# A block of three MLPs on one core: SBUF tiles at other addresses, and the MLP's first matrices with the high and the low part of x side by side in one 512-column matmul

## The chip, the core and the metric

The kernel runs on one core of a Trainium2 chip. The metric is the device time of one execution in microseconds (us), the median of several runs.

## The reference

One token block of 256 rows and 1024 columns in float32 passes through three layers. The first has a convolution branch, a stick-breaking attention and a cross attention to a memory, and then an MLP; the other two have attention, retention and an MLP. The three MLPs compute the same form, and the change's new matmuls are in them alone:

```python
h2 = rms_norm(x, g_mlp[l])
x = x + jnp.square(jax.nn.relu(h2 @ w_up[l])) @ w_down[l]
...
hid = jnp.square(jax.nn.relu(jnp.einsum('bsd,df->bsf', x, w_ff1)))
ff = jnp.einsum('bsf,fd->bsd', hid, w_ff2)
return layernorm(DEEPNORM_ALPHA * x + ff, ln2_g, ln2_b)
```

The first matrix (`w_up`, `w_ff1`) is 1024 x 4096, the second (`w_down`, `w_ff2`) 4096 x 1024.

## The kernel before, in words

**Three matmuls for one product.** Each operand is split into a high part (rounded to float32r, by ACT) and a low part (what is left, by DVE). A product is high x high + high x low + low x high: `mm3`, lines 319 to 322, so the trace shows each product as three matmuls, of lines 320, 321 and 322. The names in a matmul's row are the moving operand first and the weights (the stationary operand) second: `acc<-xTh,whi` streams `xTh` past weights from `whi`.

**Weights come as a stream.** `Stream` (lines 164 to 232) walks a fixed plan of 196 chunks of 1024 x 256 or 512 x 512 weights. A chunk comes in two halves: a DMA of 512 KB into one of five `raw` buffers (`load`, line 190, on SP's queue), a cast by ACT to `whi` (line 213) and a subtraction by DVE to `wlo` (line 214). There are five buffers of each, and in the MLPs a sixth pair that is lent (`lend`). `tick` puts one half (`pump`) in the order of ACT and DVE after each unit of matmuls, so that three chunks or more lie ahead of PE. The order on each engine is the order of the program text; no scheduler changes it.

**Two shapes of unit.** `unit_b` (line 340) has the activations as weights and streams 512 columns of `whi` or `wlo`: 4 steps of k, 12 matmuls of 512 columns. `unit_a` (line 335) has a 128 x 128 block of `whi` or `wlo` as weights and streams the 256 tokens of `xTh` or `xTl`: 8 steps of k, 24 matmuls of 256 columns. `stream_a` (line 347) does two such units, the halves of one PSUM bank `acc` (four banks go round).

**An MLP** (`mlp`, line 789): the first 1024 columns of the first matrix go by `unit_b`. Then for each group g from 2 to 7 there are two chunks of the first matrix by `stream_a`; ACT takes relu out of the bank and squares (lines 800, 801), `split` (line 311) makes the two parts of `hid[g]`, and four units `down` of the second matrix use `hid[g - 2]`. A program has 36 such chunks, 3 x 6 x 2, with 36 x 2 x 8 = 576 products of 256 columns.

**Where tiles lie.** Pools are stacked from low addresses (side "left") or from the top (side "right"), each tile on a multiple of 32 bytes. In the kernel before, small tiles of 4 to 96 bytes stand ahead of large ones. The starts (bytes in a partition) as the built programs have them, and what is left of them after division by 256:

| tiles | before | rest | changed | rest |
|---|---|---|---|---|
| `whi`, five, 8448 apart | 38176 | 32 | 17408 | 0 |
| `wlo`, five, 8448 apart | 80416 | 32 | 59648 | 0 |
| lent `whi`, `wlo` | 182176, 190624 | 160 | 180736, 189184 | 0 |
| `xTh`, `xTl` (changed: one `xT`) | 130848, 139040 | 32 | 110080 | 0 |
| `hid`, `ych`, `memTh`, `mTh`, `osbh`, `oxh` and their low parts | from 149408 | 160 | from 147968 | 0 |
| `mixh`, `mixl` | 149440, 157632 | 192 | 147968, 156160 | 0 |
| `ident` (moving operand of transposes) | 16512 | 128 | 16896 | 0 |

A step of k moves an operand by 1024 or 2048 bytes, which keeps the rest, but for 96 matmuls of 264 columns (k steps of 1056 bytes). Counted in the program before, among float32r matmuls of 128 rows: of 2,936 with 512 columns, 1,247 stream an operand with the same rest as the weights that the next matmul needs, and 1,689 one with another; 3,418 have 256 columns (1,728 of them in the 576 products above). No moving operand of float32r starts on a multiple of 128 bytes, but for some of those with 264 columns.

Of the kernel before, what the change touches and what calls it, by code (L numbers as in the profile page):

```python
# [9 lines left out]
F32 = mybir.dt.float32  # L10
F32R = mybir.dt.float32r
# [9 lines left out]
RB = 5  # L21
# [218 lines left out]
def block_kernel(ctx: ExitStack, tc: tile.TileContext, a: dict, out: bass.AP, upto=None, dbg=None):  # L240
# [3 lines left out]
    def pool(stack, name, bufs=1, side="left", space=None):  # L244
        kw = {} if space is None else {"space": space}
        return stack.enter_context(tc.tile_pool(name=name, bufs=bufs, side=side, reuse_waits="tile", **kw))

    kp = pool(ctx, "const")
    rp = pool(ctx, "raw", RB)
    wp = pool(ctx, "wts", NB)  # L250
    ap = pool(ctx, "act")
    accp = pool(ctx, "acc", 4, space=bass.MemoryType.PSUM)
    psum = ExitStack()
    ctx.push(psum)
    cur_ps = [None]
    sm = pool(ctx, "small", 4)

    def acc():
        return accp.tile([128, 512], F32, tag="acc", name="acc")
# [80 lines left out]
    def unit_b(o, w, t, x, k0=0, first=True, last=True):  # L340
        nk = w[0].shape[1]
        ts = slice(t * 128, t * 128 + 128)
        for k in range(nk):
            mm3(o, x[0][:, k0 + k, ts], x[1][:, k0 + k, ts], w[0][:, k, :], w[1][:, k, :],
                first and k == 0, last and k == nk - 1)

    def stream_a(key, x):
        w = W.get(key)
        p = acc()
        pv = p.rearrange("p (n t) -> p n t", n=2)  # L350
        unit_a(pv[:, 0, :], w, 0, x)
# [27 lines left out]
        (nc.sync, nc.scalar)[h].dma_start(xt[:, 0, 512 * h:512 * h + 512], xsrc[:, 0, 512 * h:512 * h + 512])  # L379
    gmix = ph0.tile([128, D], F32, name="gmix")  # L380
    nc.sync.dma_start(gmix, a["g_mix"][0].partition_broadcast(128))
    ident = kp.tile([128, 128], F32, name="ident")
    nc.scalar.dma_start(ident, a["c1"][:, 0:128])
    W.load(2)
    nc.sync.dma_start(xt[:, 1, :], xsrc[:, 1, :])
    W.load()
    mh = kp.tile([128, 4], F32, name="mh")
    nc.gpsimd.memset(mh, -0.5)
    wz = ph0.tile([128, 512], BF16, name="wz")
    nc.vector.memset(wz, 0.0)  # L390
# [26 lines left out]
        stt(dst, src, rs, gb, ALU.mult, ALU.mult)  # L417

    def new_xT():
        return (ap.tile([128, 8, S], F32R, tag="xTh", name="xTh"), ap.tile([128, 8, S], F32R, tag="xTl", name="xTl"))  # L420


    hT = new_xT()
    ht = [ph0.tile([128, D], F32, name=f"ht{t}") for t in range(2)]
    ss = sm.tile([128, 2], F32, tag="ss2", name="ss2")
    rs = sm.tile([128, 1], F32, tag="rs", name="rs")
    for h in range(2):
        hs = slice(512 * h, 512 * h + 512)
# [46 lines left out]
    dmask = sp.tile([128, 128], F32, name="dmask")  # L475
    nc.gpsimd.dma_start(smask, a["c1"][:, 128:896])
    nc.gpsimd.dma_start(dmask, a["c1"][:, 896:1024])
    cw = sp.tile([128, 8, 3], F32, name="cw")
    nc.gpsimd.dma_start(cw, a["conv_w"])
    qs = tuple(sp.tile([128, 2, S], F32R, name=f"q{i}") for i in range(2))  # L480
    kb = tuple(sp.tile([128, 2, S], F32R, name=f"kb{i}") for i in range(2))
    u = sp.tile([128, 2, S + 2], F32, name="u")
    nc.vector.memset(u[:, :, 0:2], 0.0)

    yc = ycur("yc")
# [261 lines left out]
    def rms_half(t, n, bank, xtok, gb, dst, xT, cell):  # L747
        ns = slice(512 * n, 512 * n + 512)
        if n == 0:
            cell[t] = sm.tile([128, 2], F32, tag="ss2", name="ss2")  # L750
        tt(xtok[:, t, ns], bank, xtok[:, t, ns], ALU.add)
        nc.scalar.activation(dst[:, ns], xtok[:, t, ns], AF.Square, accum_out=cell[t][:, n:n + 1])
        if n == 1:
            ss = sm.tile([128, 1], F32, tag="ss", name="ss")
            rs = sm.tile([128, 1], F32, tag="rs", name="rs")
            tt(ss, cell[t][:, 0:1], cell[t][:, 1:2], ALU.add)
            rstd_of(rs, ss, 1, 1.0 / D, EPS)
            stt(dst, xtok[:, t, :], rs, gb, ALU.mult, ALU.mult)
            sides.append(late_T(dst, xT, t))
# [29 lines left out]
    def mlp(tag, xT, half, on_start):  # L789
        st = ExitStack()  # L790
        tmp = lambda: hp.tile([128, D], F32, tag="r", name="r", bufs=2)
        hp = pool(st, "mlp" + str(tag))
        W.lend(pool(st, "wts" + str(tag)), (tag, "dn", 7, 1))
        hid = {}

        def new_hid(g):
            hid[g] = tuple(hp.tile([128, 4, S], F32R, tag=f"hid{i}", name=f"hid{i}", bufs=3) for i in range(2))

        def relu2(dst, src):
            nc.scalar.activation(dst, src, AF.Relu)  # L800
# [12 lines left out]
        ws = [(n, j, W.get((tag, "up", n, j))) for n in range(2) for j in range(2)]
        new_hid(0)
        new_hid(1)
        for t in range(2):
            p = [bank(), bank()]
            r = hp.tile([128, D], F32, tag="r", name="r", bufs=2)
            for n, j, w in ws:
                unit_b(p[n], w, t, xT, 4 * j, j == 0, j == 1)  # L820
                if t == 1:
                    W.free()
                if j:
                    relu2(r[:, 512 * n:512 * n + 512], p[n])
                    if n:
                        sides.append(tok_side(t, r))
                tick(1)
            if t == 0:
                on_start(st)
        pd = None  # L830

        def down(g, n, t, w):
            unit_b(pd[t][n], w, t, hid[g], 0, g == 0, g == 7)

        for g in range(2, 8):
            new_hid(g)
            for cc in range(2):
                p = stream_a((tag, "up", 2 * g + cc), xT)
                r = hp.tile([128, D], F32, tag="r", name="r", bufs=2)
                rv = r[:, 0:512].rearrange("p (n t) -> p n t", n=2)  # L840
                relu2(rv, p)
                split(hid[g][0][:, 2 * cc:2 * cc + 2, :], hid[g][1][:, 2 * cc:2 * cc + 2, :], rv)
                tick()
            if pd is None:
                pd = [[bank(), bank()] for _ in range(2)]
            for n in range(2):
                w = W.get((tag, "dn", g - 2, n))
                for t in range(2):
                    down(g - 2, n, t, w)
                    if t == 1:  # L850
                        W.free()
                    tick()
        ws = [(W.get((tag, "dn", g, n)), g, n) for n in range(2) for g in (6, 7)]
        for t in range(2):
            for w, g, n in ws:
                down(g, n, t, w)
                if t == 1:
                    W.free()
                if g == 7:
                    half(t, n, pd[t][n], tmp)  # L860
# [17 lines left out]

    def open_b2(st):
        st4.close()  # L880
        cp = pool(b2, "c2", side="right")
        for nm, sh, dt in (("cst", [128, C2W], F32), ("sel", [128, 8, 128], F32R), ("chl", [128, S], F32R),
                           ("gnp", [128, 2, 4], F32)):
            c2s[nm] = cp.tile(sh, dt, name=nm)
# [27 lines left out]
    def ln_half(t, n, bank, xtok, gb, bb, xT, cell, tmp, fin=None):  # L912
        ns = slice(512 * n, 512 * n + 512)
        if n == 0:
            cell[t] = sm.tile([128, 2], F32, tag="lsum", name="lsum")
        nc.vector.scalar_tensor_tensor(out=xtok[:, t, ns], in0=xtok[:, t, ns], scalar=ALPHA, in1=bank, op0=ALU.mult,
                                       op1=ALU.add, accum_out=cell[t][:, n:n + 1])
        if n == 0:
            return
        nm = sm.tile([128, 1], F32, tag="nm", name="nm")  # L920
        ss = sm.tile([128, 1], F32, tag="ss", name="ss")
        rs = sm.tile([128, 1], F32, tag="rs", name="rs")
        nc.vector.tensor_scalar(nm, cell[t][:, 0:1], cell[t][:, 1:2], -1.0 / D, op0=ALU.add, op1=ALU.mult)
# [14 lines left out]
    for l in range(2):  # L938
# [3 lines left out]
        def T(shape, dt, tag, bufs=1):  # L942
            return p2.tile(shape, dt, tag=tag, name=tag, bufs=bufs)

        bf = T([128, 8], F32, "bf")
        nc.gpsimd.dma_start(bf, a["b_forget_2"][l].partition_broadcast(128))
        mix = (T([128, 8, S], F32R, "mixh"), T([128, 8, S], F32R, "mixl"))


        qr = T([128, 2, 512], F32, "ta")  # L950
        kr = T([128, 2, 512], F32, "tb")
        fy = T([128, 2, 8], F32, "fy")

        def rotary(dst, src, t):
            nh = src.shape[1] // 128
# [34 lines left out]
           cc_("zeta").unsqueeze(2).to_broadcast([128, 4, 128]), ALU.mult)  # L990


        fa = T([128, 2, 8], F32, "fa")
        act_set(EXPLN)
        nc.scalar.activation(fa, fy, AF.Abs)
        nc.scalar.activation(fa, fa, AF.Exp, scale=-1.0)
# [48 lines left out]
        def fox_pair(g, nt, z_at, e_at, t_at, pv_at):  # L1045
# [10 lines left out]
                    mm(zb[:, h, :], sel[64 * h:64 * h + 40, 2 * pair + h, :], chl[64 * h:64 * h + 40, 0:nk], False, True)  # L1056
            zd = z[:, :, 128:384].rearrange("p h (b k) -> p h b k", b=2)
            tt(zd, zd, cc_("neg").unsqueeze(1).unsqueeze(1).to_broadcast([128, 2, 2, 128]), ALU.add)
            mx = sm.tile([128, 4], F32, tag="fmx", name="fmx")
            nc.vector.tensor_reduce(mx[:, 0:2], z[:, :, 0:256], AX.X, ALU.max)  # L1060
            nc.vector.tensor_reduce(mx[:, 2:4], z[:, :, 256:384], AX.X, ALU.max)
            nc.vector.tensor_scalar(mx, mx, -1.0, None, op0=ALU.mult)
# [62 lines left out]
        def ret_side():  # L1125
# [139 lines left out]
```

## Time and profile before

| what | value |
|---|---|
| median of 3 runs | 1223.83 us (1223.82 to 1224.01) |
| profiled execution | 1223.95 us, span 1222.1 us |
| PE busy | 1208.5 us, 99% of the span, 7365 matmuls |
| DVE busy | 734.8 us, 60% |
| ACT busy | 631.6 us, 52% |
| HBM | 178 GB/s over the span |
| chain that ended last | PE 95% |

The span is the time from the first to the last instruction; the execution's own time is 1.85 us longer. A matmul's row in the trace has a start and a duration; the durations overlap (a matmul of 256 columns lasts 0.28 us and the next starts 0.12 us after it), so the pace is read from the distance of starts.

### The profile page before, as it was taken

Reading aid. Unit: us, or ns where it says so; the run is one execution under the profiler, and the core shown is the slowest. Engines: PE = TensorE matmul, PEld = TensorE weight load, DVE = VectorE, ACT = ScalarE, POOL = GpSimd, SP = SyncE. Lnnn points to the kernel's source line nnn. Section 1 sums busy time; section 2 is a strip of 40 time slices with the busy share of each in tenths; the row PEclk is TensorE's granted clock in tenths of the full one; section 3 lists DMA queues with packets and bytes.
Section 4 is the critical chain, followed back from the end, with each engine's and each line's share of the span. In section 5 each row is a group of like instructions: output and inputs, shape, how many; then the busy total and the mean of one; then the engine's idle time right before and its main releaser. Section 6 shows DMA issues by size and latency. Waiting matters only on the chain.

```text
span 1222.1 us, 18186 instructions
## 1 busy us (share of the span) xinstructions
PE 1208.5 (99%) x7365; PEld 1059.1 (87%) x7365; DVE 734.8 (60%) x941; ACT 631.6 (52%) x887; POOL 26.2 (2%) x45
## 2 busy tenths in 40 slices
PE   8999999999999999999999999999999999999997
PEld 5999987887888888998898889899889888989985
DVE  6488775656666655355476685535567668553452
ACT  6556555545454565455255556545535555653540
POOL 1000000000000000000000100000000010000000
PEclk9999999999999999999999999999999999999999
DMA  8644446665455565556444366555545436655530
GB/s 327 224 148 144 140 156 211 233 195 162 138 172 189 184 243 208 172 172 214 156 166 139 124 214 226 197 188 173 207 130 187 146 118 216 225 193 203 167 126 35
DMA packets 60468, 218.99 MB, mean 179 GB/s; under 512 B 6848, under 2 KB 6992, under 8 KB 60384
## 3 DMA queue, kind: packets, MB, share of 16 engines
q1 hardware_dynamic: 58320, 211.12, 51.6%
q0 software_dynamic: 1776, 6.38, 1.8%
q8 instruction: 58, 0.95, 0.3%
q10 hardware_dynamic: 288, 0.33, 0.1%
q14 instruction: 26, 0.21, 0.0%
HBM read 216.75 MB, written 1.05 MB: 178 GB/s over the span
## 4 chain that ended last, share of the span: by engine, by line
PE 95%; DVE 1%; ACT 1%; DMA 1%; issue 0%; DVEq 0%; POOLq 0%; SPq 0%; ACTq 0%
PE acc L320 17%; PE acc L322 17%; PE acc L321 17%; PE bank L320 13%; PE bank L322 13%; PE bank L321 13%; PE acc L402 2%; PE acc L333 2%; PE aux L329 1%; DMA raw<-in_wpack_dram 1%; PE aux L1082 0%; DMA gmix<-in_g_mix_dram 0%; DVE wlo L214 0%; PE aux L515 0%; PE aux L322 0%
## 5 line engine op out<-in xcount | busy, mean ns | idle before, releaser
L214 DVE TENSOR_TENSOR wlo<-raw,whi 128x1024 fp32r<-128x1024 f32 x392 | 465.0, 1221 | 116.6 <-ACT whi L213 114.5
L213 ACT CAST whi<-raw 128x1024 fp32r<-128x1024 f32 x392 | 394.6, 1048 | 108.7 <-PE bank L322 58.0
L320 PE MATMUL acc<-xTh,whi 128*128 128x256 f32 x1088 | 310.6, 285 | 0.0
L321 PE MATMUL acc<-xTl,whi 128*128 128x256 f32 x1088 | 307.7, 283 | 0.0
L322 PE MATMUL acc<-xTh,wlo 128*128 128x256 f32 x1088 | 307.5, 283 | 0.0
L320 PEld LDWEIGHTS acc<-xTh,whi 128*128 128x128 f32 x1088 | 207.9, 191 | 2.7 <-issue 1.0
L321 PEld LDWEIGHTS acc<-xTl,whi 128*128 128x128 f32 x1088 | 207.9, 191 | 1.0
L322 PEld LDWEIGHTS acc<-xTh,wlo 128*128 128x128 f32 x1088 | 208.0, 191 | 0.0
L320 PE MATMUL bank<-whi,hid 128*128 128x512 f32 x384 | 151.4, 394 | 0.0
L322 PE MATMUL bank<-whi,hid 128*128 128x512 f32 x384 | 151.3, 394 | 0.0
L321 PE MATMUL bank<-wlo,hid 128*128 128x512 f32 x384 | 151.2, 394 | 0.0
L306 DVE TENSOR_TENSOR hid<-r,hid 128x512 fp32r<-128x512 f32 x36 | 24.9, 692 | 166.2 <-ACT hid L312 166.2
L800 ACT ACTIVATE r<-acc 128x512 f32<-128x512 f32 x36 | 21.5, 598 | 147.1 <-PE acc L322 147.1
L320 PE MATMUL acc<-whi,xTh 128*128 128x512 f32 x224 | 90.6, 404 | 0.7 <-ACT xTh L312 0.7
L321 PE MATMUL acc<-wlo,xTh 128*128 128x512 f32 x224 | 88.2, 394 | 1.1 <-DVE wlo L214 1.1
L322 PE MATMUL acc<-whi,xTl 128*128 128x512 f32 x224 | 88.3, 394 | 0.0
L322 PEld LDWEIGHTS bank<-whi,hid 128*128 128x128 f32 x384 | 72.2, 188 | 16.9
L320 PEld LDWEIGHTS bank<-whi,hid 128*128 128x128 f32 x384 | 72.3, 188 | 15.9
L321 PEld LDWEIGHTS bank<-wlo,hid 128*128 128x128 f32 x384 | 72.2, 188 | 16.0
L320 PE MATMUL bank<-whi,xTh 128*128 128x512 f32 (+2 forms) x192 | 68.7, 358 | 0.0
L321 PE MATMUL bank<-wlo,xTh 128*128 128x512 f32 (+2 forms) x192 | 68.1, 354 | 0.0
L322 PE MATMUL bank<-whi,xTl 128*128 128x512 f32 (+2 forms) x192 | 68.0, 354 | 0.0
(263 smaller groups left out, 1457.6 us busy)
## 6 DMA issues: line engine op xcount, KB each, us to landing
raw<-in_wpack_dram SPq DMA_DIRECT2D x388, 512.0 KB, 4.4
raw<-in_wpack_dram SPq DMA_DIRECT2D x4, 528.0 KB, 4.3
gb<-in_ln_g_dram POOLq DMA_DIRECT2D x4, 512.0 KB, 3.9
bb<-in_ln_b_dram POOLq DMA_DIRECT2D x4, 512.0 KB, 6.1
x<-in_x_dram SPq DMA_DIRECT2D x3, 512.0 KB, 7.0
mem<-in_mem_dram SPq DMA_DIRECT2D x2, 512.0 KB, 6.5
out_dram<-x SPq DMA_DIRECT2D x4, 256.0 KB, 2.2
cst<-in_c_dram POOLq DMA_DIRECT2D x1, 898.0 KB, 7.0
```

What stands on the lines that cost most here:

```text
L213: nc.scalar.copy(hi, raw)
L214: nc.vector.tensor_tensor(lo, raw, hi.bitcast(F32), op=ALU.subtract)
L306: nc.vector.tensor_tensor(o, x, y, op=op)
L320: nc.tensor.matmul(o, lhsT=lh, rhs=rh, start=first, stop=False, skip_group_check=True)
L321: nc.tensor.matmul(o, lhsT=lh, rhs=rl, start=False, stop=False, skip_group_check=True)
L322: nc.tensor.matmul(o, lhsT=ll, rhs=rh, start=False, stop=last, skip_group_check=True)
L329: nc.tensor.matmul(o[:, h, :], lhsT=q[a][hs[h]], rhs=k[b][hs[h]], start=i == 0, stop=i == 2, skip_group_check=True)
L333: nc.tensor.matmul(o, lhsT=l, rhs=r, start=first, stop=last, skip_group_check=True)
L402: nc.tensor.transpose(o[:, k * 128:(k + 1) * 128], src[:, k * 128:(k + 1) * 128], ident)
L800: nc.scalar.activation(dst, src, AF.Relu)
```

## The change

It does two things. First, the pools and small tiles are put in another order, with padding, so that each large tile starts on a multiple of 256 bytes; small tiles go to the top of SBUF. Second, `xTh` and `xTl` become one tile `xT` with the high and the low part of a k step side by side, and a new `stream_w` takes the place of `stream_a` in the MLPs: for each k, one matmul streams both parts, 512 columns, past the high part of the weights, and one streams the high part, 256 columns, past the low part. So a half chunk fills a bank by itself, and DVE adds the bank's two halves into `r` (a `tensor_reduce` over two elements that lie 256 apart). The relu then reads `r`.

```diff
     kp = pool(ctx, "const")
-    rp = pool(ctx, "raw", RB)
+    mh = kp.tile([128, 4], F32, name="mh")
+    kp.tile([128, 88], F32, name="pad0")
+    ident = kp.tile([128, 128], F32, name="ident")
     wp = pool(ctx, "wts", NB)
     ap = pool(ctx, "act")
+    rp = pool(ctx, "raw", RB)
+    rp.tile([128, 96], F32, name="pad1", bufs=1)
...
-    sm = pool(ctx, "small", 4)
+    sm = pool(ctx, "small", 4, side="right")
...
+    def stream_w(key, x, evict):
+        w = W.get(key)
+        for nt in range(2):
+            p = acc()
+            ns = slice(nt * 128, nt * 128 + 128)
+            for k in range(8):
+                wide = lambda: mm(p.rearrange("p (s t) -> p s t", s=2), w[0][:, k, ns], x[2][:, k], k == 0, k == 7)
+                if k < 7:
+                    wide()
+                mm(p[:, 0:S], w[1][:, k, ns], x[0][:, k, :], False, False)
+                if k == 7:
+                    wide()
+            if nt:
+                W.free()
+            evict(nt, p.rearrange("p (s t) -> p t s", s=2))
+            if not nt:
+                tick()
...
     def new_xT():
-        return (ap.tile([128, 8, S], F32R, tag="xTh", name="xTh"), ap.tile([128, 8, S], F32R, tag="xTl", name="xTl"))
+        xT = ap.tile([128, 8, 2, S], F32R, tag="xT", name="xT")
+        return xT[:, :, 0, :], xT[:, :, 1, :], xT
...
-                p = stream_a((tag, "up", 2 * g + cc), xT)
                 r = hp.tile([128, D], F32, tag="r", name="r", bufs=2)
                 rv = r[:, 0:512].rearrange("p (n t) -> p n t", n=2)
-                relu2(rv, p)
+                stream_w((tag, "up", 2 * g + cc), xT, 
+                         lambda nt, h: nc.vector.tensor_reduce(rv[:, nt, :], h, AX.X, ALU.add))
+                relu2(rv, rv)
```

The rest of the diff moves small tiles (`bf`, `fy`, `fa`, the statistics of the norms and of the attention) to pools at the top of SBUF, and `cw` behind `u`.

On PE, where the first `stream_a` of the first MLP begins, the program before has (moving operand, then weights):

```order
L321 MATMUL bank<-wlo,xTh 128x512
L322 MATMUL bank<-whi,xTl 128x512
L320 MATMUL acc<-xTh,whi 128x256
L321 MATMUL acc<-xTl,whi 128x256
L322 MATMUL acc<-xTh,wlo 128x256
L320 MATMUL acc<-xTh,whi 128x256
```

and the changed program has, around the end of the first half chunk (its last k has the narrow matmul first):

```order
L338 MATMUL acc<-xT,whi 128x512
L338 MATMUL acc<-xT,wlo 128x256
L338 MATMUL acc<-xT,whi 128x512
L338 MATMUL acc<-xT,wlo 128x256 x2
L338 MATMUL acc<-xT,whi 128x512 x2
L338 MATMUL acc<-xT,wlo 128x256
```

Three matmuls of 256 columns have become one of 512 and one of 256; there are 576 matmuls and 576 weight loads fewer.

On DVE, in the same group of the first MLP, the program before has:

```order
L214 TENSOR_TENSOR wlo<-raw,whi 128x1024 x3
L306 TENSOR_TENSOR hid_4083<-r,hid_4082 128x512
L214 TENSOR_TENSOR wlo<-raw,whi 128x1024
L306 TENSOR_TENSOR hid_3879<-acc,hid_3878 128x4x128
L306 TENSOR_TENSOR hid_3881<-acc,hid_3880 128x4x128
L214 TENSOR_TENSOR wlo<-raw,whi 128x1024
L306 TENSOR_TENSOR hid_4083<-r,hid_4082 128x512
```

and the changed program:

```order
L214 TENSOR_TENSOR wlo<-raw,whi 128x1024 x2
L867 TENSOR_REDUCE r<-acc 128x256
L214 TENSOR_TENSOR wlo<-raw,whi 128x1024
L867 TENSOR_REDUCE r<-acc 128x256
L311 TENSOR_TENSOR hid_4088<-r,hid_4087 128x512
L214 TENSOR_TENSOR wlo<-raw,whi 128x1024
L867 TENSOR_REDUCE r<-acc 128x256
```

Each half chunk has brought a reduction that waits for PE, with a half of a later weight chunk behind it. The orders of ACT, POOL and SP are as they were, but for names.

## Rows read from the trace of the kernel before

**Rows 1.** The page: busy time, granted clock in 40 slices, chain by engine.

```profile
PE 1208.5 (99%) x7365; PEld 1059.1 (87%) x7365; DVE 734.8 (60%) x941; ACT 631.6 (52%) x887; POOL 26.2 (2%) x45
...
PEclk9999999999999999999999999999999999999999
...
PE 95%; DVE 1%; ACT 1%; DMA 1%; issue 0%; DVEq 0%; POOLq 0%; SPq 0%; ACTq 0%
```

**Rows 2.** Two windows: stretch and length, busy by engine, granted clock, DMA share, GB/s.

```profile
10.60:13.10 2.50, 2.50 (x6) 1.78 (x6) 2.42 (x5) 2.50 (x4) 0.00 (x0) 0.50 1.02 416
446.00:604.00 158.00, 158.00 (x964) 141.14 (x963) 77.67 (x75) 79.30 (x97) 0.54 (x1) 1.00 0.53 181
```

**Rows 3.** Timeline of PE, one chunk by `stream_a`: start us, duration us, instruction.

```profile
488.25 0.28 PE L320 MATMUL acc<-xTh,whi 128*128 128x256 f32 x1
...
499.63 0.28 PE L322 MATMUL acc<-xTh,wlo 128*128 128x256 f32 x1
499.75 0.39 PE L320 MATMUL bank<-whi,hid 128*128 128x512 f32 x1
```

**Rows 4.** Timeline of PE, `unit_b` with weights from `xTh` and `xTl`.

```profile
418.52 0.39 PE L320 MATMUL bank<-whi,xTh 128*128 128x512 f32 x1
...
423.96 0.39 PE L320 MATMUL bank<-whi,xTh 128*128 128x512 f32 x1
```

**Rows 5.** Timeline of PE, `down`: first from lent buffers, from 505.21 from others.

```profile
502.27 0.39 PE L322 MATMUL bank<-whi,hid 128*128 128x512 f32 x1
...
504.99 0.39 PE L322 MATMUL bank<-whi,hid 128*128 128x512 f32 x1
505.21 0.40 PE L320 MATMUL bank<-whi,hid 128*128 128x512 f32 x1
...
508.01 0.40 PE L320 MATMUL bank<-whi,hid 128*128 128x512 f32 x1
```

**Rows 6.** Timeline of PE, the matmuls of 264 columns.

```profile
613.96 0.28 PE L320 MATMUL bank<-whi,xTh 128*128 128x264 f32 x1
...
616.86 0.28 PE L320 MATMUL bank<-whi,xTh 128*128 128x256 f32 x1
```

**Rows 7.** Timeline of PE, the start, inside the first window of rows 2.

```profile
11.88 0.63 PE L320 MATMUL acc<-whi,xTh 128*128 128x512 f32 x1
...
13.16 0.48 PE L320 MATMUL acc<-whi,xTh 128*128 128x512 f32 x1
```

**Rows 8.** The chain: start us, us, what (eight transposes with `ident` moving).

```profile
426.86 0.87 PE acc L402 x8
```

**Rows 9.** Groups by line, 455.1 to 477.7 us (one group g), DVE: count, busy, mean ns, idle.

```profile
L214 DVE TENSOR_TENSOR wlo<-raw,whi 128x1024 fp32r<-128x1024 f32 x8 | 9.3, 1220 | 0.7 <-ACT whi L213 0.7
L306 DVE TENSOR_TENSOR hid<-r,hid 128x512 fp32r<-128x512 f32 x2 | 1.4, 694 | 10.3 <-ACT hid L312 10.3
```

**Rows 10.** Groups by line, whole span, DVE: a reduction out of PSUM.

```profile
L1060 DVE TENSOR_REDUCE fmx<-aux 128x2 f32<-128x512 f32 x8 | 5.5, 691 | 0.3
```

More of the change, by code (lines that the diff above doesn't have):

```diff
@@ L381, in block_kernel @@
     nc.sync.dma_start(gmix, a["g_mix"][0].partition_broadcast(128))
-    ident = kp.tile([128, 128], F32, name="ident")
     nc.scalar.dma_start(ident, a["c1"][:, 0:128])
@@ L386, in block_kernel @@
     W.load()
-    mh = kp.tile([128, 4], F32, name="mh")
     nc.gpsimd.memset(mh, -0.5)
@@ L419, in new_xT @@
     def new_xT():
-        return (ap.tile([128, 8, S], F32R, tag="xTh", name="xTh"), ap.tile([128, 8, S], F32R, tag="xTl", name="xTl"))
+        xT = ap.tile([128, 8, 2, S], F32R, tag="xT", name="xT")
+        return xT[:, :, 0, :], xT[:, :, 1, :], xT
     hT = new_xT()
     ht = [ph0.tile([128, D], F32, name=f"ht{t}") for t in range(2)]
-    ss = sm.tile([128, 2], F32, tag="ss2", name="ss2")
+    ss = sm.tile([128, 2], F32, tag="ss2", name="ss2", bufs=3)
     rs = sm.tile([128, 1], F32, tag="rs", name="rs")
@@ L477, in block_kernel @@
     nc.gpsimd.dma_start(dmask, a["c1"][:, 896:1024])
-    cw = sp.tile([128, 8, 3], F32, name="cw")
-    nc.gpsimd.dma_start(cw, a["conv_w"])
     qs = tuple(sp.tile([128, 2, S], F32R, name=f"q{i}") for i in range(2))
     kb = tuple(sp.tile([128, 2, S], F32R, name=f"kb{i}") for i in range(2))
-    u = sp.tile([128, 2, S + 2], F32, name="u")
+    u = sp.tile([128, 2 * (S + 2)], F32, name="u").rearrange("p (n s) -> p n s", n=2)
+    cw = sp.tile([128, 8, 3], F32, name="cw")
+    sp.tile([128, 96], F32, name="pad2")
+    nc.gpsimd.dma_start(cw, a["conv_w"])
     nc.vector.memset(u[:, :, 0:2], 0.0)
@@ L749, in rms_half @@
         if n == 0:
-            cell[t] = sm.tile([128, 2], F32, tag="ss2", name="ss2")
+            cell[t] = sm.tile([128, 2], F32, tag="ss2", name="ss2", bufs=3)
         tt(xtok[:, t, ns], bank, xtok[:, t, ns], ALU.add)
@@ L880, in open_b2 @@
         st4.close()
[L881 to L884, printed above, removed]
+        cp = pool(b2, "c2", 4, side="right")
+        for nm, sh, dt in (("sel", [128, 8, 128], F32R), ("chl", [128, S], F32R), ("cst", [128, C2W], F32),
+                           ("gnp", [128, 2, 4], F32), ("pad3", [128, 36], F32)):
+            c2s[nm] = cp.tile(sh, dt, name=nm, bufs=1)
+        for nm, sh in (("bf", [128, 8]), ("fy", [128, 2, 8]), ("fa", [128, 2, 8])):
+            c2s[nm] = cp.tile(sh, F32, name=nm, bufs=1)
+        c2s["small"] = cp
         selr = pool(selst, "selr", side="right").tile([128, 8, 128], F32, name="selr")
@@ L914, in ln_half @@
         if n == 0:
-            cell[t] = sm.tile([128, 2], F32, tag="lsum", name="lsum")
+            cell[t] = c2s["small"].tile([128, 2], F32, tag="lsum", name="lsum")
         nc.vector.scalar_tensor_tensor(out=xtok[:, t, ns], in0=xtok[:, t, ns], scalar=ALPHA, in1=bank, op0=ALU.mult,
@@ L919, in ln_half @@
             return
-        nm = sm.tile([128, 1], F32, tag="nm", name="nm")
+        nm = c2s["small"].tile([128, 1], F32, tag="nm", name="nm")
         ss = sm.tile([128, 1], F32, tag="ss", name="ss")
@@ L943, in T @@
             return p2.tile(shape, dt, tag=tag, name=tag, bufs=bufs)
-        bf = T([128, 8], F32, "bf")
+        bf = c2s["bf"]
         nc.gpsimd.dma_start(bf, a["b_forget_2"][l].partition_broadcast(128))
@@ L951, in block_kernel @@
         kr = T([128, 2, 512], F32, "tb")
-        fy = T([128, 2, 8], F32, "fy")
+        fy = c2s["fy"]
         def rotary(dst, src, t):
@@ L990, in block_kernel @@
            cc_("zeta").unsqueeze(2).to_broadcast([128, 4, 128]), ALU.mult)
-        fa = T([128, 2, 8], F32, "fa")
+        fa = c2s["fa"]
         act_set(EXPLN)
@@ L1058, in fox_pair @@
             tt(zd, zd, cc_("neg").unsqueeze(1).unsqueeze(1).to_broadcast([128, 2, 2, 128]), ALU.add)
-            mx = sm.tile([128, 4], F32, tag="fmx", name="fmx")
+            mx = c2s["small"].tile([128, 4], F32, tag="fmx", name="fmx")
             nc.vector.tensor_reduce(mx[:, 0:2], z[:, :, 0:256], AX.X, ALU.max)
@@ L1066, in fox_pair @@
             e = fp.tile([128, 2, 384], F32, tag="fe", name="fe")
-            su = sm.tile([128, 4], F32, tag="fsu", name="fsu")
+            su = c2s["small"].tile([128, 4], F32, tag="fsu", name="fsu")
             act_set(EXPLN)
@@ L1142, in ret_side @@
                 p = ps[t]
-                bst = sm.tile([128, 4, 6], F32, tag="gst", name="gst")
-                mv = sm.tile([128, 4, 2], F32, tag="gmv", name="gmv")
-                rs = sm.tile([128, 4], F32, tag="grs", name="grs")
+                bst = c2s["small"].tile([128, 4, 6], F32, tag="gst", name="gst")
+                mv = c2s["small"].tile([128, 4, 2], F32, tag="gmv", name="gmv")
+                rs = c2s["small"].tile([128, 4], F32, tag="grs", name="grs")
                 for h in range(4):
```

## The prediction

> **What bounds the kernel now.** I read the page first. PE is busy for 1208.5 of 1222.1 us, the chain that ended last is PE for 95%, and the granted clock is full in every slice but the ends [rows 1]. In the window of a whole MLP, PE has no gap: 158.00 of 158.00 us, with DVE at 49% and ACT at 50% [rows 2]. So time comes or goes by the distance between the starts of PE's matmuls, and next I read that from the timeline.
>
> The `stream_a` units: 96 matmuls of 256 columns from 488.25 to 499.75, 119.8 ns each [rows 3]. At the full clock, 2.4 GHz, 256 columns are 106.7 ns; 13.1 ns are over. The 512-column matmuls have two paces. With weights from `xTh` and `xTl`: 24 from 418.52 to 423.96, 226.7 ns, 13.3 over the 213.3 of their columns [rows 4]. With weights from `hid`: 12 from 502.27 to 504.99, 226.7 ns; and right behind them, same line, same tiles but for the weight buffer that is streamed, 12 from 505.21 to 508.01, 233.3 ns [rows 5]. The first set streams the lent buffers, whose start leaves the rest 160 after division by 256, as `hid` does; the second streams buffers with the rest 32 against 160 for `hid`. With `xTh` it is 32 against 32. So equal rests go with 226.7 and unequal ones with 233.3, a step of 6.6 ns.
>
> What of the 13 ns that are left at equal rests? Two rows speak. While the clock was at half, 1.2 GHz [rows 2], three matmuls of 512 columns came 426.7 ns apart [rows 7], which is 512 columns and nothing over. And the matmuls of 264 columns come at 120.8 ns, 24 from 613.96 to 616.86 [rows 6]: eight columns more than 256 cost 1.0 ns, not 3.3. A fixed extra of 13.2 would give 123.2. Blocks of 32 columns (128 bytes) fit better: tiles at rest 32 begin eight columns into such a block, so 512 columns touch 17 blocks, 256 touch 9, and 264 touch 9 at each of their starts. At 13.33 ns a block that is 226.7, 120.0 and 120.0. That reading is mine, from these paces alone; no row has a full-rate matmul of 256 or 512 columns that starts on a block.
>
> **The change, part by part.**
>
> *The layout.* All large tiles now start on multiples of 256 bytes, so all rests are equal, and 512 columns touch 16 blocks and 256 touch 8. The pace then lies between that of the columns alone (213.3 and 106.7) and that of today at equal rests (226.7 and 119.8). Below, the nearest row is the transposes: eight in 0.87 us, 109 ns each [rows 8], whose moving operand `ident` is the only one on a block's start, each with its own weight load. I take 109.0 for 256 columns, as they need a weight load each too, and the same 2.3 over the columns for 512: 215.6.
> - 512 columns, equal rests now: 1,247 x (226.7 - 215.6) = 13.8 us.
> - 512 columns, unequal rests now: 1,689 x (233.3 - 215.6) = 29.9 us.
> - 256 columns outside the products that change form, 1,690 x (119.8 - 109.0) = 18.3 us.
> - The 96 matmuls of 264 columns touch 9 blocks as before: nothing.
>
> The Trainium skill, page "TensorE: Matmul & The Clock Gate", section "Wait — 56ns, not 53.3ns?", gives a warm matmul a fixed cost of about 2.5 ns over its columns. The paces above do not agree: 13.1 and 13.3 over. If 2.5 were all that could be had back per matmul, the layout would be worth little, and the merge of two matmuls below 576 x 2.5 = 1.4 us by that page.
>
> *Wide and narrow.* In 576 products, three matmuls of 256 columns (3 x 119.8 = 359.4 ns) become one of 512 and one of 256: 215.6 + 109.0 = 324.6. That is 576 x 34.8 = 20.0 us. Of this, the merge alone, at today's paces, is 359.4 - 226.7 - 119.8 = 12.9 ns each, 7.4 us: one surplus of 13 less.
>
> *DVE's reductions.* 72 are added. The nearest row reads 512 elements of PSUM in 691 ns [rows 10]; I take 0.69 each, with 0.4 and 1.22 (as long as a `wlo` subtraction [rows 9]) as ends. A group g has four: 2.8 us more on top of 9.3 + 1.4 [rows 9], so 13.5 in a group of about 2 x 16 x 0.3246 + 48 x 0.2156 = 20.7 us. PE's work covers it, at the long end too (15.6 us). Each waits for PE on its half chunk, and behind it on DVE stand the halves of later chunks; those lie three chunks, over 15 us, ahead of PE. ACT's relu now waits for DVE, 0.7 us later than for PE; `hid[g]` is wanted only by the `down` two groups later. The bank is now freed by the reduction, and PE comes back to it after four units, some 8 us. So I cost all this at nothing. Were the cover gone, 72 x 0.69 = 50 us would be in play.
>
> *DMA.* SP's order is as before. The weights come in a span 7% shorter, so the mean rate goes up by 7%, from 181 GB/s in the MLP's window; the start had 416 in its window [rows 2]. Hidden.
>
> *What is late next.* PE's idle time, 13.6 us, lies at the ends and stays. In the attention parts PE's short steps wait for ACT and DVE, whose instructions do not get faster while PE does; between 0 and 8 us of new waits, and I take 4, the middle.
>
> Sum: 13.8 + 29.9 + 18.3 + 20.0 - 4 = 78 us. From the profiled execution's 1223.95 us that gives 1146; it lies 0.1 us over the median, which I leave out. With nothing over the columns and no new waits it would be some 17 us less (5,780 matmuls x 2.3 = 13, and the 4): 1129. If a block were 64 bytes long, half of the surplus would stay (220.0 and 113.3): 8.4 + 22.5 + 11.0 + 15.0 = 57 us, 1167. A difference under 0.2%, 2.4 us, is about what a measurement of this kernel cannot tell from none.
>
> **The rivals.**
>
> 1. *The 13 ns stay.* The surplus is a cost of switching weights, whatever the address, and the layout only makes unequal rests equal. For it: it is nearly the same at 256 and at 512. Against: 264 columns at 120.8, and no surplus at the half clock, where a fixed cost in PE cycles would show as 27 ns. Time: 1,689 x 6.6 = 11.1, and 576 x 12.9 = 7.4, so 18.5 us: 1205.
>
> 2. *The layout does nothing.* The 6.6 ns come from something else that goes with the lent buffers, and the paces do not follow addresses. Then the merge alone is left, with the wide matmul at 226.7 to 233.3: 576 x 6.3 to 12.9 = 3.6 to 7.4 us, 1217 to 1220. Beside it stands a rule of the Trainium skill, page "TensorE: Matmul & The Clock Gate", section "Step-by-step: what each phase is for": loading the next weights takes nothing from the running matmul's reads of SBUF, as each has a port of its own. By that rule the rests of two operands could not matter. Against rival 2 speak [rows 4, 5]: the two neighbouring units above differ in the weight buffer alone, and `xTh`, with yet other tiles, has the pace that its rest asks for.
>
> 3. *Slower: both streams at a block's start collide.* Equal rests were seen at 32 and at 160, never at 0. If reads of moving operand and weights that cross blocks at once get in each other's way there, the step of 6.6 that unequal rests cost comes on top of the slower paces: 239.9 and 126.4. Time: 1,247 x 13.2 + 1,689 x 6.6 + 1,690 x 6.6 + 576 x 6.9 = 16.5 + 11.1 + 11.2 + 4.0 = 43 us more, 1267. It turns to a loss as soon as the pace of 512 columns at rest 0 passes about 232. Against: the two equal rests that exist are the good ones.
>
> 4. *No difference*: rival 2 with DVE's waits eating the rest, a few us each way.
>
> **How the numbers follow.** Forecast and its half-surplus variant (1129 to 1170) 0.63; rival 1 (about 1205) 0.21; rival 2 (1217 to 1220) 0.07; rival 4 0.03; rival 3 0.06. Faster than by 2.4 us are the forecast and rivals 1 and 2: 0.91; same 0.03; slower 0.06. The range has to hold the forecast and rival 1, 0.84 together, less a little of the low end: 1135 to 1209. The forecast's own range is 1135 to 1170. The two cases stand apart, and a result between 1170 and 1200 is not expected by any.
>
> **What would show it.** Right: starts of 256-column matmuls 109 apart, of 512 columns 216 wherever they stand, also in `down`; a k step of `stream_w` 325; matmuls of 264 columns still near 121; DVE near 60% + 50 us, PE still 98% busy. If `down` shows 227 everywhere and a k step 346, rival 1 holds; if 227 and 233 stay side by side, rival 2. PE idle in front of matmuls into `acc`, released by the reduction, would show my zero for DVE wrong.

## The result, and the profile after

The changed kernel takes 1210.25 us (median of 4 runs, 1210.06 to 1210.45); beside it the kernel before took 1223.91. The ratio is 0.9888, 95% interval 0.9871 to 0.9905: faster by 13.7 us, where 78 were forecast. The time lies just outside the range, near rival 1 (1205).

From the page of the changed kernel (span; busy time; chain by engine; four of the groups by line):

```profile
span 1208.4 us, 17123 instructions
PE 1193.5 (99%) x6789; PEld 1027.7 (85%) x6789; DVE 779.6 (65%) x1013; ACT 632.7 (52%) x887; POOL 26.1 (2%) x45
PE 95%; DVE 2%; ACT 1%; DMA 1%; issue 0%; DVEq 0%; POOLq 0%; SPq 0%; ACTq 0%
L338 PE MATMUL acc<-xT,whi 128*128 128x512 f32 x576 | 201.2, 398 | 0.0
L338 PE MATMUL acc<-xT,wlo 128*128 128x256 f32 x576 | 149.8, 281 | 0.0
L826 ACT ACTIVATE r<-r 128x512 f32<-128x512 f32 x36 | 22.8, 633 | 151.1 <-DVE r L867 151.1
L867 DVE TENSOR_REDUCE r<-acc 128x256 f32<-128x512 f32 x72 | 49.5, 687 | 57.3 <-PE acc L338 57.3
```

Two windows of its MLPs (columns as in [rows 2]):

```profile
436.00:594.00 158.00, 158.00 (x796) 133.93 (x795) 93.46 (x100) 81.14 (x101) 0.00 (x0) 1.00 0.57 190
742.00:900.00 158.00, 158.00 (x797) 134.01 (x796) 96.70 (x111) 80.41 (x100) 0.56 (x1) 1.00 0.56 185
```

PE has as few gaps as before: 158.00 of 158.00 us, with DVE up from 77.67 us [rows 2] to 93.46. ACT's relu now waits for DVE's reduction instead of PE, 151.1 us in total, and PE waits for neither: its waits in the profile all lie outside the three MLPs. PE is busy 15.0 us less than in [rows 1], and its idle time is 1.3 us more. So the answer again lies in the distances between starts.

PE's timeline: `down`, then the first products by `stream_w`:

```profile
474.67 0.39 PE L326 MATMUL bank<-wlo,hid 128*128 128x512 f32 x1
...
484.42 0.39 PE L327 MATMUL bank<-whi,hid 128*128 128x512 f32 x1
484.64 0.39 PE L338 MATMUL acc<-xT,whi 128*128 128x512 f32 x1
484.87 0.28 PE L338 MATMUL acc<-xT,wlo 128*128 128x256 f32 x1
484.99 0.40 PE L338 MATMUL acc<-xT,whi 128*128 128x512 f32 x1
485.22 0.28 PE L338 MATMUL acc<-xT,wlo 128*128 128x256 f32 x1
485.33 0.40 PE L338 MATMUL acc<-xT,whi 128*128 128x512 f32 x1
485.58 0.28 PE L338 MATMUL acc<-xT,wlo 128*128 128x256 f32 x1
485.70 0.40 PE L338 MATMUL acc<-xT,whi 128*128 128x512 f32 x1
```

`down`: 43 distances in 9.75 us, 226.7 ns each; the 233.3 of [rows 5] is gone, but nothing near 215.6 has come. Over the whole trace, where two 512-column matmuls follow one another, the mean distance (waits left out) went from 231.8 to 226.9 with weights from `hid`, from 232.7 to 227.9 with `memT` and from 233.3 to 227.4 with `mix`. With weights from `xT`, whose rest was equal before too, it stayed: 228.1 and 227.9. The same timeline where `stream_a` is left, and at the 264-column matmuls:

```profile
99.78 0.28 PE L325 MATMUL acc<-xT,whi 128*128 128x256 f32 x1
...
103.62 0.28 PE L327 MATMUL acc<-xT,wlo 128*128 128x256 f32 x1
...
608.11 0.28 PE L325 MATMUL bank<-whi,xT 128*128 128x264 f32 x1
...
610.89 0.28 PE L327 MATMUL bank<-whi,xT 128*128 128x264 f32 x1
```

32 distances in 3.84 us are 120.0 ns, as in [rows 3]; 23 in 2.78 us are 120.9, as in [rows 6]. And one row of the chain, the two chunks of a group by `stream_w` (32 wide and 32 narrow matmuls):

```profile
484.81 11.28 PE acc L338 x64
```

That is 352.5 ns for a wide and a narrow matmul, against 3 x 119.8 = 359.4 before: 6.9 ns less, times 576 = 4.0 us. Over the 512-column matmuls outside `stream_w`, the distances add up to 9.8 us less than before. Together 13.8 us; the span is shorter by 13.7.

### The profile page after: what moved, and what is told of

It is laid out like the page before. It is cut to its first block, busy times and chain, and to the rows that moved or that the text cites. A ratio compares the mean times of both kernels' runs of the same rounds, so it can differ in the third digit from the quotient of the medians.

```text
span 1208.4 us, 17123 instructions
## 1 busy us (share of the span) xinstructions
PE 1193.5 (99%) x6789; PEld 1027.7 (85%) x6789; DVE 779.6 (65%) x1013; ACT 632.7 (52%) x887; POOL 26.1 (2%) x45
## 4 chain that ended last, share of the span: by engine, by line
PE 95%; DVE 2%; ACT 1%; DMA 1%; issue 0%; DVEq 0%; POOLq 0%; SPq 0%; ACTq 0%
PE acc L338 19%; PE bank L325 13%; PE bank L327 13%; PE bank L326 13%; PE acc L325 11%; PE acc L326 11%; PE acc L327 11%; PE acc L425 2%; PE aux L334 1%; DMA raw<-in_wpack_dram 1%; DMA gmix<-in_g_mix_dram 0%; PE aux L1112 0%; DVE wlo L214 0%; PE aux L541 0%; PE aux L327 0%
## 5 line engine op out<-in xcount | busy, mean ns | idle before, releaser
L214 DVE TENSOR_TENSOR wlo<-raw,whi 128x1024 fp32r<-128x1024 f32 x392 | 466.8, 1221 | 102.1 <-ACT whi L213 100.2
L338 PE MATMUL acc<-xT,whi 128*128 128x512 f32 x576 | 201.2, 398 | 0.0
L338 PE MATMUL acc<-xT,wlo 128*128 128x256 f32 x576 | 149.8, 281 | 0.0
L325 PE MATMUL acc<-xT,whi 128*128 128x256 f32 x512 | 147.6, 288 | 0.0
L326 PE MATMUL acc<-xT,whi 128*128 128x256 f32 x512 | 144.8, 283 | 0.0
L327 PE MATMUL acc<-xT,wlo 128*128 128x256 f32 x512 | 144.7, 283 | 0.0
L338 PEld LDWEIGHTS acc<-xT,whi 128*128 128x128 f32 x576 | 104.8, 188 | 20.3
L338 PEld LDWEIGHTS acc<-xT,wlo 128*128 128x128 f32 x576 | 108.7, 189 | 6.5
L826 ACT ACTIVATE r<-r 128x512 f32<-128x512 f32 x36 | 22.8, 633 | 151.1 <-DVE r L867 151.1
L325 PEld LDWEIGHTS acc<-xT,whi 128*128 128x128 f32 x512 | 98.0, 191 | 1.9 <-issue 1.0
L326 PEld LDWEIGHTS acc<-xT,whi 128*128 128x128 f32 x512 | 98.1, 192 | 0.2
L327 PEld LDWEIGHTS acc<-xT,wlo 128*128 128x128 f32 x512 | 98.0, 191 | 0.0
L325 PE MATMUL acc<-whi,xT 128*128 128x512 f32 x224 | 90.3, 403 | 0.9 <-ACT xT L317 0.9
L326 PE MATMUL acc<-wlo,xT 128*128 128x512 f32 x224 | 88.4, 394 | 1.1 <-DVE wlo L214 1.1
L327 PE MATMUL acc<-whi,xT 128*128 128x512 f32 x224 | 88.2, 394 | 0.0
L867 DVE TENSOR_REDUCE r<-acc 128x256 f32<-128x512 f32 x72 | 49.5, 687 | 57.3 <-PE acc L338 57.3
L327 PEld LDWEIGHTS bank<-whi,hid 128*128 128x128 f32 x384 | 72.1, 188 | 15.1
```

Of the source, the lines that this page charges most:

```text
L214: nc.vector.tensor_tensor(lo, raw, hi.bitcast(F32), op=ALU.subtract)
L325: nc.tensor.matmul(o, lhsT=lh, rhs=rh, start=first, stop=False, skip_group_check=True)
L326: nc.tensor.matmul(o, lhsT=lh, rhs=rl, start=False, stop=False, skip_group_check=True)
L327: nc.tensor.matmul(o, lhsT=ll, rhs=rh, start=False, stop=last, skip_group_check=True)
L338: nc.tensor.matmul(o, lhsT=l, rhs=r, start=first, stop=last, skip_group_check=True)
L867: lambda nt, h: nc.vector.tensor_reduce(rv[:, nt, :], h, AX.X, ALU.add))
```

## The experiments

**Theory A**: a float32r matmul keeps its surplus of 13 ns at every address; equal rests give 226.7 and unequal ones 233.3. Its rivals: the rests are nothing and the merge gave everything, or the merge spoils what the layout gives.

### The layout alone

In the changed kernel, the up chunks go back to `stream_a`, without reductions:

```diff
+                p = stream_a((tag, "up", 2 * g + cc), xT)
...
-                stream_w((tag, "up", 2 * g + cc), xT, 
-                         lambda nt, h: nc.vector.tensor_reduce(rv[:, nt, :], h, AX.X, ALU.add))
-                relu2(rv, rv)
+                relu2(rv, p)
```

> The changed kernel with its layout, but the MLP's products by three matmuls of 256 columns as before. Theory A (what the layout brings is only that the moving operand and the next weights now have the same rest after division by 256): the 1,689 matmuls of 512 columns that came at 232 to 233 ns come at 227, all else stays, about 10 us less than before: 1213 to 1215 us. Theory B (the address does nothing, the gain is the merge alone): 1223 to 1224. My forecast's blocks of 32 columns: over 60 us less.

Measured: 1214.65 us, ratio 0.9925 (0.9913 to 0.9938), 9.0 us faster than before. Theory A had 1213 to 1215, the forecast's blocks over 60 us less.

### The merge alone

In the kernel before, `xT` as one tile and `stream_w` in the up chunks, the pools left as they were:

```diff
...
-        return (ap.tile([128, 8, S], F32R, tag="xTh", name="xTh"), ap.tile([128, 8, S], F32R, tag="xTl", name="xTl"))
+        xT = ap.tile([128, 8, 2, S], F32R, tag="xT", name="xT")
+        return xT[:, :, 0, :], xT[:, :, 1, :], xT
...
-                p = stream_a((tag, "up", 2 * g + cc), xT)
...
-                relu2(rv, p)
+                stream_w((tag, "up", 2 * g + cc), xT, 
+                         lambda nt, h: nc.vector.tensor_reduce(rv[:, nt, :], h, AX.X, ALU.add))
+                relu2(rv, rv)
```

> The kernel before with its layout, and only the wide and narrow matmuls with DVE's reductions. Theory A: the pair costs what it costs in the changed kernel, 352.5 ns against 359.4, since xT and the weights had equal rests before: 576 x 6.9 = 4 us less than before, about 1220 us. Theory B: all of the changed kernel's gain, 1210. If layout and merge depend on each other, the gains of this run and of the layout alone don't add up to 13.7 us.

Measured: 1219.03 us, ratio 0.9961 (0.9948 to 0.9973), 4.6 us faster. The two parts, 9.0 and 4.6, add up to the whole: neither needs the other, nor spoils it.

### Other tiles half a step off

In the changed kernel, 128 bytes more in front of `hid`, the mixers' and the memory's tiles and the lent buffers; the weight buffers and `xT` stay where they are:

```diff
-    rp.tile([128, 96], F32, name="pad1", bufs=1)
+    rp.tile([128, 128], F32, name="pad1", bufs=1)
```

> The changed kernel with one padding 128 bytes longer, so that hid, mix, memT and the others of that stack start at rest 128, and the weight buffers and xT stay at 0. Theory A: their matmuls of 512 columns come at 232 to 233 again (those from the lent buffers, which move along, at 227): about 10 us more than the changed kernel, 1219 to 1221. Theory B: no difference, 1210.

Measured: 1218.48 us, ratio 0.9957 (0.9943 to 0.9970): 8.2 us of the layout's 9.0 are gone (theory A had 1219 to 1221). PE's timeline in `down` of this kernel:

```profile
479.63 0.39 PE L326 MATMUL bank<-wlo,hid 128*128 128x512 f32 x1
...
487.53 0.40 PE L327 MATMUL bank<-whi,hid 128*128 128x512 f32 x1
```

34 distances in 7.90 us, 232.4 ns. All large tiles here start on multiples of 128 bytes, so it is the inequality of the two rests that costs, not a start inside a block.

### The paces by themselves

A kernel of PE work alone (it copies x to the output and computes nothing of the reference): series of matmuls of one form, 48 each, operands at chosen rests after division by 256.

```diff
+    run(512, bm, bw)
+    run(256, bm, bw)
+    for n in (128, 192, 224, 240, 256, 264, 272, 288, 320, 384, 448, 504, 512):
+        run(n, m[0], w[0])
+    for r in (32, 64, 96, 128, 160, 192):
+        run(512, m[r], w[0])
+    for r in (32, 64, 128):
+        run(256, m[r], w[0])
+    run(512, m[32], w[32])
+    run(512, m[128], w[128])
+    run(512, m[0], w[32])
...
```

> Not the reference's computation: x is copied to the output, and PE runs 48 matmuls each of many kinds back to back, with nothing else at work. Theory A1 (a fixed cost of 13 ns at each change of float32r weights, from no address): 512 columns at 226.7 and 256 at 119.8 at rest 0, 272 columns at 126.5, and each width its columns / 2.4 GHz + 13.3; rests other than that of the weights 5 to 6 ns more. Theory A2 (a pace in steps of 32 columns): 264, 272 and 288 columns all near 120 and 320 at 133. Forecast: rest 0 at 215.6 and 109. bfloat16 at columns / 2.4 GHz + 2.5 or less. If 64 weight columns halve the 13 ns, it is a matter of loading weights. Wide and narrow in turn 352 a pair if turning costs, 346.5 if not; eight and eight 346.5.

Mean distance of starts, worked out from the trace without the first four of each series, ns:

```
float32r, both rests 0, columns: 128..224  240    256    264    272    288    320    384    448    504    512
                                 111.7     112.0  119.9  120.0  125.3  131.7  146.7  173.3  206.7  226.9  226.8
512 columns, weights at rest 0, moving at rest:  32     64     96     128    160    192
                                                 233.3  228.9  233.5  233.4  234.2  233.4
512 columns, both at rest 32: 226.7; both at 128: 227.3; moving 0, weights 32: 233.4
256 columns, moving at rest 32, 64, 128: 117.8 to 118.5
bfloat16: 512 columns 215.8, 256 columns 109.2
```

This settles the step of the forecast that failed. With both operands at rest 0, on the start of a block of 128 or of 256 bytes, 512 columns keep 226.8 and 256 keep 119.9. The row that had spoken for blocks of 32 columns, 264 columns at 120.8 [rows 6], comes out at 120.0 at rest 0 too: the pace does not grow evenly with the width (264 as 256, 512 as 504). Both theories of this run missed as well: by A1 (the columns and 13.3 ns) 264 columns would come at 123.3 and 448 at 200.0, and unequal rests would cost 5 to 6 ns at 256 columns too; by A2 (steps of 32 columns) 272 and 288 would come near 120 and 320 at 133. And the surplus differs by type: bfloat16 has 2.5 ns, float32r 13 (it has twice the bytes in a column too; no run takes the two apart).

### Wide and narrow in groups

The 352.5 ns are 5.8 more than 226.7 + 120.0. In the trace most wide starts stand 233 to 241 ns before the next one, the narrow ones 113 to 120. If turning from one width to the other costs this, fewer turns give it back. In the changed kernel, per half chunk, eight wide ones and then eight narrow ones:

```diff
-                wide = lambda: mm(p.rearrange("p (s t) -> p s t", s=2), w[0][:, k, ns], x[2][:, k], k == 0, k == 7)
-                if k < 7:
-                    wide()
-                mm(p[:, 0:S], w[1][:, k, ns], x[0][:, k, :], False, False)
-                if k == 7:
-                    wide()
+                mm(p.rearrange("p (s t) -> p s t", s=2), w[0][:, k, ns], x[2][:, k], k == 0, False)
+            for k in range(8):
+                mm(p[:, 0:S], w[1][:, k, ns], x[0][:, k, :], False, k == 7)
```

> The changed kernel with the eight wide matmuls of a half chunk first and the eight narrow ones behind them. Theory W1 (turning from wide to narrow and back costs the 6 ns by which a pair is over 226.7 + 119.8): paces of the run of paces give about 2793 ns a half chunk in place of 2820, 72 x 27 = 1.9 us less than the changed kernel: 1208.3; at full rate from the first one, 2772, 3.4 us less: 1206.8. Theory W2 (a wide matmul costs 233 to 241 in this place, whatever stands beside it, for its two parts or its whole bank): no change, 1210.2.

Measured: 1208.21 us, ratio 0.9874 (0.9859 to 0.9888). And two wide, two narrow in turn, from the changed kernel too (the added lines):

```diff
+            for k in range(0, 8, 2):
+                for j in (k, k + 1):
+                    mm(p.rearrange("p (s t) -> p s t", s=2), w[0][:, j, ns], x[2][:, j], j == 0, False)
+                for j in (k, k + 1):
+                    mm(p[:, 0:S], w[1][:, j, ns], x[0][:, j, :], False, j == 7)
```

> The same with two wide and two narrow matmuls in turn. Theory W1: half the turns, so about half of the 6 ns come back on each pair: 576 x 3 = 1.7 us less than the changed kernel, 1208.5. Theory W2: 1210.2.

Measured: 1207.84 us, ratio 0.9871 (0.9854 to 0.9887), the fastest kernel of this study. Theory W1 (the turns cost) had 1208.3 and 1208.5, theory W2 (a wide matmul costs the same whatever stands beside it) 1210.2 for both. The intervals of these ratios and of the changed kernel's overlap, but the runs lie apart (1207.63 to 1207.94 against 1210.06 to 1210.45, where the kernel before took 1223.60 beside the one and 1223.91 beside the other), and the chain of the pairs' kernel shows the gain in its place:

```profile
484.52 11.14 PE acc L338 x64
```

11.14 us where the changed kernel has 11.28: over 18 groups 2.5 us.

### What the surplus hangs on

Again PE work alone, with each series in weights of its own, so that the timeline has a row for each. `mov` is at rest 0, `off` at rest 128, all weights at rest 0:

```diff
+    run((512,), mov, w["wa"])
+    run((256,), mov, w["wb"])
...
+    run((512,), off, w["wf"])
+    run((512,), mov, w["wg"], cols=64)
+    run((256,), mov, w["wh"], cols=64)
...
+    run((512, 256), mov, w["wk"], 48)
+    run((512, 512, 256, 256), mov, w["wl"], 24)
+    run((512,) * 4 + (256,) * 4, mov, w["wm"], 12)
+    run((512,) * 8 + (256,) * 8, mov, w["wn"], 6)
...
+    run((512, 256), off, w["wp"], 48)
+    run((512,), mov, w["wa"])
```

> Not the reference's computation: x is copied to the output, and PE runs rows of matmuls back to back, each row with weights of its own name. Surplus from loading weights (theory L): with 64 or 32 weight columns in place of 128 the surplus over 256 columns falls from 13 to 7 and 3 ns, and 128 columns come no faster than the load itself, 112 ns. Fixed surplus at each change (theory F): the weight columns make no difference, 119.8 and 226.7 each time. Moving operand at rest 128: 233. Pairs of wide and narrow: 352; two and two, four and four, eight and eight in between that and 346.5, falling with the size of the group if turning costs.

PE's timeline (a series is one row; its pace is the distance to the next row's start over the count):

```profile
51.86 5.92 PE L54 MATMUL acc<-mov,wb 128*128 128x256 f32 x48
57.61 5.93 PE L54 MATMUL acc<-mov,wc 128*128 128x264 f32 x48
63.38 7.20 PE L54 MATMUL acc<-mov,wd 128*128 128x320 f32 x48
70.42 5.47 PE L54 MATMUL acc<-mov,we 128*128 128x128 f32 x48
75.72 11.37 PE L54 MATMUL acc<-off,wf 128*128 128x512 f32 x48
86.92 11.21 PE L54 MATMUL acc<-mov,wg 128*64 128x512 f32 x48
97.98 5.63 PE L54 MATMUL acc<-mov,wh 128*64 128x256 f32 x48
103.44 11.28 PE L54 MATMUL acc<-mov,wi 128*32 128x512 f32 x48
114.56 5.62 PE L54 MATMUL acc<-mov,wj 128*32 128x256 f32 x48
120.01 17.12 PE L54 MATMUL acc<-mov,wk 128*128 128x512 f32 x96
136.97 16.88 PE L54 MATMUL acc<-mov,wl 128*128 128x512 f32 x96
153.69 17.00 PE L54 MATMUL acc<-mov,wm 128*128 128x512 f32 x96
170.53 16.92 PE L54 MATMUL acc<-mov,wn 128*128 128x512 f32 x96
187.29 8.49 PE L54 MATMUL acc<-mov,wo 128*128 128x384 f32 x48
195.61 17.01 PE L54 MATMUL acc<-off,wp 128*128 128x512 f32 x96
212.46 11.07 PE L54 MATMUL acc<-mov,wa 128*128 128x512 f32 x48
```

`wb` 119.8, `wc` 120.2, `wd` 146.7, `we` 110.4, and 512 columns at unequal rests (`wf`) 233.3: the series before is confirmed. With 64 and 32 columns of weights, 256 columns fall to 113.8 and 113.5, but 512 columns do not fall, 230.4 and 231.7. So neither "the surplus is the loading of weights" nor "a fixed price per change of weights" holds for both widths; what the surplus is stays open. The mixtures per wide and narrow pair: in turn 353.3 (`wk`), two and two 348.3 (`wl`), four and four 350.8, eight and eight 349.2. With no other engine at work and no waits, strict turn is the dearest and two and two the cheapest, as in the kernels: the turn's price is PE's own. It does not fall steadily with fewer turns, as had been expected: four and four cost more than two and two, and why stays open. In strict turn with the moving operand at rest 128 against 0 (`wp`) a pair takes 351.0, less than the 353.3 at equal rests: what unequal rests cost a run of 512 columns, they do not cost here.

### The same form in the attention part

Last, the pairs' kernel with 20 more chunks in this form, those of the self-attention and convolution part (`sq`, `sk`, `ch`, `cc`, `cb`):

```diff
+    def stream_s(key, x):
+        r = sp.tile([128, 512], F32, tag="sa", name="sa", bufs=2)
+        rv = r.rearrange("p (n t) -> p n t", n=2)
+        stream_w(key, x, lambda nt, h: nc.vector.tensor_reduce(rv[:, nt, :], h, AX.X, ALU.add))
+        return rv
...
-        p = stream_a(("sq", i), hT)
+        p = stream_s(("sq", i), hT)
```

> The kernel of e6 (two wide, two narrow in turn), with the same form given to the 20 chunks of the self-attention and convolution part (sq, sk, ch, cc, cb) that run as three 256-column matmuls per product: 20 x 16 = 320 products, 40 more DVE reductions into a new SBUF tile. Theory P (pace of the pairs and DVE hidden): 3 x 119.8 = 359.4 ns become (233 + 235 + 117 + 113 + 232 + 231 + 113 + 120 + 233 + 236 + 116 + 112 + 233 + 230 + 114 + 119) / 8 = 348.4 ns, 11.0 ns less, 320 x 11.0 = 3.5 us: 1207.84 - 3.5 = 1204.3 us. Rival D (DVE is in the way there: it works on the attention's scans and masks at the same time): each of the 20 chunks gives its result one reduction of 0.69 us later to a step that PE waits for, 20 x 0.69 = 13.8 us: 1218, with PE idle in front of the heads' matmuls.

Measured: 1229.92 us (4 runs, 1228.88 to 1230.78), ratio 1.0048 (1.0031 to 1.0065): slower than the kernel before, and 22.1 us slower than the pairs, where theory P had 3.5 us of gain. Windows of this kernel, then of the pairs' kernel:

```profile
60.00:100.00 40.00, 35.70 (x209) 30.50 (x208) 32.65 (x40) 19.79 (x25) 0.00 (x0) 0.91 0.39 121
80.00:84.00 4.00, 0.63 (x8) 0.30 (x4) 3.94 (x4) 0.00 (x0) 0.00 (x0) 0.85 0.00 0
84.00:90.00 6.00, 5.97 (x19) 5.09 (x20) 4.95 (x6) 3.32 (x5) 0.00 (x0) 0.53 0.52 152
```

```profile
60.00:100.00 40.00, 40.00 (x343) 38.67 (x342) 32.09 (x37) 23.91 (x31) 0.00 (x0) 1.00 0.42 134
```

PE's waits in this kernel from 20 to 220 us (waiter, releaser: us in total, times, longest; the three largest):

```profile
PE acc L338 <- DVE sa L373: 10.7, 3, 3.6
PE aux L545 <- DVE r L311: 3.1, 4, 1.0
PE acc L325 <- ACT sg L591: 2.8, 1, 2.8
```

DVE's timeline ahead of the wait that ends at 84.03:

```profile
78.50 0.96 DVE L314 SCALAR_TENSOR_TENSOR e<-aux,e 128x768 f32<-128x768 f32 x1 [1.35 <-ACT e L530]
79.49 1.76 DVE L532 TENSOR_TENSOR_SCAN r<-smask,e 128x768 f32<-128x768 f32 x1
81.28 0.96 DVE L311 TENSOR_TENSOR r<-aux,r 128x768 f32<-128x768 f32 x1
82.16 1.22 DVE L214 TENSOR_TENSOR wlo<-raw,whi 128x1024 fp32r<-128x1024 f32 x1
83.29 0.68 DVE L373 TENSOR_REDUCE sa<-acc 128x256 f32<-128x512 f32 x1
```

PE's timeline, the matmuls that end it:

```profile
84.03 1.22 PE L338 MATMUL acc<-xT,whi 128*128 128x512 f32 x2 [3.40 <-DVE sa L373]
```

DVE was busy for 32.09 of 40 us there before the edit, 80%, against 49% in the MLP [rows 2]. The reduction, which alone frees the bank, stands behind the attention's scan and a weight chunk's subtraction; a half chunk now takes a bank by itself, so PE runs out of banks sooner, and it stands still for 3.4 us. Behind that the granted clock is 0.53 for 6 us, close to the lower of its two levels, 1.2 GHz. From 20 to 220 us, in five windows of 40, PE's busy time falls from 199.11 to 182.67 us, 16.4 us of standing still, and the clock means (1.00, 0.91, 0.91, 0.96, 0.96) leave out 10.4 us' worth of full clock; less the 3.5 us that theory P gives, that is 23.3, beside 22.1 measured. This is an estimate: some of the low clock falls into the standing still itself and counts twice. Rival D had the engine right and the place wrong: it put the waits in front of the heads' matmuls, and the longest stand in front of the wide ones, for want of a bank. Its 1218 left out the clock.

## Why the prediction was wrong

**The step that failed** is the reading of the 13 ns that are left at equal rests: "Blocks of 32 columns (128 bytes) fit better". At rest 0 the surplus is 13.3 ns, as at 32 and at 128. All terms that rest on 215.6 and 109.0 go with it: 13.8 us and 18.3 us measured as nothing, 29.9 as 9.8 in the trace (9.0 by the layout alone). Each of the three rows that led there could be read another way. The 264 columns were taken as blocks at an address; they are a step in the width. The half clock without a surplus [rows 7] was held against a fixed cost; but the Trainium skill, page "TensorE: Matmul & The Clock Gate", section "Wait — 56ns, not 53.3ns?", says of its fixed 2.5 ns too that it shows only at the full clock, so this row could not tell the two apart. Of the 2.5 ns themselves: the trace agrees for bfloat16 (215.8 and 109.2), not for float32r (226.8 and 119.9). And the transposes at 109 ns [rows 8] are of 128 columns, where float32r too has 111.7 up to 240 columns: a floor, not the pace of 256.

**Rival 1** had what happens, at a chance of 0.21: the 13 ns stay and unequal rests become equal. Its reason for the 13 ns, a cost of switching weights, no run shows: the paces by width and by columns of weights fit no fixed price. Its 1205 was low in two sizes. Unequal rests gave 9.0 us (the layout alone) for the 11.1 of 1,689 x 6.6, since over the whole trace they fell by about 5 ns each (231.8 to 226.9 with `hid`). The merge gave 6.9 ns a product for 12.9, because a wide matmul between narrow ones does not run at 226.7: most of its starts stand 233 to 241 ns before the next.

**Wide and narrow**, 20.0 us: measured 4.0 in the changed kernel, 4.6 by itself.

**The rests** were right in kind: equal ones 226.7, unequal ones 232 to 234, at any start tried but 64 against 0 (228.9). The Trainium skill, page "TensorE: Matmul & The Clock Gate", section "Step-by-step: what each phase is for", lets the loading of weights take nothing from the moving operand's reads; at 512 columns of float32r no run here bears that out, since the rest of the one against the other costs 6.6 ns (233.3 against 226.7).

**DVE at nothing** was right: 687 ns for the 691 taken, PE never waits for a reduction in the MLP. The attention part shows what the zero rested on: a DVE that is busy for half of its time, as in the MLP, and not for 80%.

**Smaller terms.** The half-surplus case (1167) leaves out the 4 us of new waits that the forecast has; with them it is 1171, one past the 1170 that it was given. 264 columns, SP's order and the DMA's higher rate cost nothing, as said. New waits, 4 us, were 1.3. Rival 3, a collision at rest 0, did not come: 226.8 there.

## What to carry to other kernels

Before a surplus over the columns is put down to addresses, measure one aligned case by itself: here that series alone would have shown 226.8 and 119.9. Where PE is the bound and matmuls in float32r stream 512 columns one after another, give moving operand and weights the same start modulo 256 bytes, and do not turn between widths at every matmul. Fewer matmuls bought with an eviction on another engine are worth it only where that engine has room (49% busy bore it here, 80% did not; nothing between was run), since the eviction frees the bank only after all that stands ahead of it.

## What the runs showed of the hardware

- Matmuls in float32r with 128 columns of weights come about 13.3 ns over their columns apart at 256, 320, 384 and 512 columns, but 10.0 over at 264, 16.9 at 504 and 20.0 at 448, and up to 240 columns 110 to 112 ns apart whatever their width.
- At 256 columns unequal rests cost nothing (117.8 to 118.5, even less than the 119.9 at equal ones); at 512 they cost 6.5 to 7.4 ns (2.1 with 64 against 0), and in strict turn with 256 nothing (351.0 a pair against 353.3).
- Wide and narrow in strict turn cost 353.3 ns a pair, two and two 348.3, four and four 350.8, eight and eight 349.2, though the sum of the two paces is 346.7.
- A stand of PE of 3.4 us was followed by 6 us at a granted clock of 0.53.
